# A position-bias table made in five steps instead of two, its rows repeated from DRAM instead of from SBUF

## The chip, the cores and the metric

The kernel runs on one core of a Trainium2 chip. The metric is the device time of one execution in microseconds (us); less is better. A measurement is the median of several executions, and beside it one execution was recorded by the hardware profiler. Engines are named as in the profile: PE (matrix products), PEld (its weight loads), DVE (vector), ACT (scalar), POOL (GpSimd), SP (the queue from which every transfer of this kernel is issued).

## The reference

Two layers on one sequence of 256 positions with 2048 features, all in float32. Layer 0 mixes the positions with an RWKV-7 recurrence, layer 1 with a causal differential attention of 8 heads; behind each mixer stands a gated MLP of width 5504 with a short convolution on its gate. After every part the input is scaled, added and normalised. The attention adds to its scores a bias that depends only on the distance of query and key:

```python
dist = (start + jnp.arange(Q_BLOCK))[:, None] - k_pos[None, :]
bias = jnp.transpose(rel_bias[rel_bucket(dist)], (2, 0, 1))
s = s + bias[None, :, None].astype(jnp.float32)
s = jnp.where(dist >= 0, s, -1e30)
```

`rel_bias` has 32 rows (buckets of distance) and 8 columns (heads).

```python
def conv_glu(x, w_up, conv_w, conv_b, w_down):
    u, g = jnp.split(x @ w_up, 2, axis=-1)
    ...
    return (u * jax.nn.gelu(gc)) @ w_down
```

## The kernel before

Activations stand transposed: a feature block of 128 lies on the partitions, the 256 positions along them, so `X` is 16 blocks of 128x256 (`KT` = 16). The order of the parts is fixed: RWKV, first MLP (`glu(0)`), attention, second MLP. Weights are read from DRAM once, in blocks made on the host so that one output block's weights are contiguous.

**A product.** `dense` makes one output block. Its weights come in transfers of four 128x128 tiles, `raw` (L204, 128 rows of 2 KB). ACT rounds two tiles at a time to a short format (`hi`, L210), DVE takes the rest (`lo`, L213), and PE multiplies each tile twice (L225 with `hi`, 512 columns; L226 with `lo`, 256 columns). In the MLP there are two pools in turn, each with 3 buffers for `raw`, 4 for `hi` and 4 for `lo`: that is how far the loads can run ahead of PE. SP issues a `raw` when the buffer that it goes into has been read by ACT and DVE.

**The MLP.** The first product (`ff_up`) makes the 43 blocks of `hs`. The second (`ff_down`) is the loop at L553: for j = 0 to 15 one output block of 43 tiles, taken in by `ln_add`, which adds it to `X` and starts the normalisation. After the first two blocks a mean is taken on PE (L394).

**The bias table.** `bias_table` is a generator that the loop advances by one step before block 1 and before block 4. It loads constants (`ext`, L173, and `rel`, L583). One small product on PE (L585) makes `tab`, 8 rows (one a head) of 384 values, one for each distance; DVE copies it from PSUM (L587). Then every row is written 128 times into the DRAM tile `dtab` (L590), and the table `B` is read back with a step of 383 between partitions (L593), which turns each repeated row into a matrix that is skewed by one position from partition to partition. The first step ends here. The second makes the small factors `nlam` and `sub` (a product at L599, an exponential at L601). The attention reads `B` at L653.

**What sets the order.** The kernel is written with a framework that places tiles, makes every semaphore and orders the instructions of each engine: program order is the priority, but an instruction whose inputs and buffers are ready can be put ahead of one that is not. On SP all instructions are carried out in the order so found, and one that waits holds up those behind it.

Of the kernel before, what the change touches and what calls it, by code (L numbers as in the profile page):

```python
# [8 lines left out]
F32 = mybir.dt.float32  # L9
# [5 lines left out]
P = 128  # L15
# [5 lines left out]
NH = 8  # L21
# [104 lines left out]
class Trunk:  # L126
# [374 lines left out]
    def glu(self, i, lead, ahead=None, out=None):  # L501
        nc, tc = self.nc, self.tc
        with ExitStack() as ctx:
            self.weight_pools(ctx, f"g{i}")
            self.psum_pool(ctx, f"g{i}", 5)
            hp = ctx.enter_context(tc.tile_pool(name=f"glu_h{i}", bufs=1))
            gp_ = ctx.enter_context(tc.tile_pool(name=f"glu_t{i}", bufs=2))
            hs = hp.tile([P, FT, 2 * T], F32R, name="hs")
            gps = [hp.tile([P, T + 2], F32, name=f"gp{k}") for k in range(2)]
            for g in gps:  # L510
                nc.gpsimd.memset(g[:, 0:2], 0.0)
            cpar = hp.tile([P, 4 * FT], F32, name="cpar")
            nc.sync.dma_start(out=cpar, in_=self.a["par"][:, PCOL[f"cw{i}0"]:PCOL[f"cw{i}0"] + 4 * FT])
            cw = lambda k, j: cpar[:, k * FT + j:k * FT + j + 1]
            state = {}

            def evac(idx, ps):
                j = idx // 2
                if idx % 2 == 0:
                    g = gps[j % 2]  # L520
                    self.total(ps, g[:, 2:])
                    gc = gp_.tile([P, T], F32, name="gc")
                    nc.vector.tensor_scalar(out=gc, in0=g[:, 0:T], scalar1=cw(0, j),
                                            scalar2=cw(3, j), op0=ALU.mult, op1=ALU.add)
                    for k in (1, 2):
                        nc.vector.scalar_tensor_tensor(out=gc, in0=g[:, k:k + T], scalar=cw(k, j),
                                                       in1=gc, op0=ALU.mult, op1=ALU.add)
                    nc.scalar.activation(out=gc, in_=gc, func=AF.Gelu_apprx_tanh)
                    state[j] = gc
                else:  # L530
                    u = gp_.tile([P, T], F32, name="u")
                    self.total(ps, u)
                    nc.vector.tensor_tensor(out=u, in0=u, in1=state.pop(j), op=ALU.mult)
                    self.split(u, hs[:, j, :])

            blocks = self.up_blocks(i)
            n = 0
            if lead:
                n = len(lead.src)
                rest = lead.run(evac, [self.psum() for _ in lead.src])  # L540
                next(rest)
                if LEAD["e"] == 0:
                    _all(rest)
            for j, w in enumerate(blocks[n:]):
                def ev(_, ps, j=j):
                    if lead:
                        for _ in range(LEAD["e"]):
                            next(rest, None)
                    evac(j + n, ps)
                self.dense([w], KT, self.S0, ev)  # L550
            todo = self.bias_table() if i == 0 else iter(())
            self.ln_begin(ahead)
            for j in range(KT):  # L553
                if j in (1, 4):
                    next(todo, None)
                last = j == KT - 1
                self.dense([self.a["ff_down"][i][j]], FT, hs, lambda _, ps: self.ln_add(j, ps, narrow=last, last=last),
                           narrow=last)
            if out is not None:
                self.ln_stats()  # L560
                self.ln_finish(i, 1, out)
            elif not ahead:
                self.ln_plain(i, 1)
# [12 lines left out]
    def bias_table(self):  # L576

        nc, tc = self.nc, self.tc
        with tc.tile_pool(name="bt", bufs=1) as bp, tc.tile_pool(name="bd", bufs=1, space=bass.MemoryType.DRAM) as dp:
            self.extra(bp, CRW, NCONST)  # L580
            rel = bp.tile([NB + 1, NH], F32, name="rel")
            nc.gpsimd.memset(rel[NB:NB + 1, :], -1e30)
            nc.sync.dma_start(out=rel[:NB, :], in_=self.a["rel_bias"])  # L583
            ps = self.psum()
            nc.tensor.matmul(ps[:NH, :384], lhsT=rel, rhs=self.x("onehot", 384, NB + 1), start=True, stop=True)  # L585
            tab = bp.tile([NH, 384], F32, name="tab")
            nc.vector.tensor_copy(out=tab, in_=ps[:NH, :384])  # L587

            dt = dp.tile([NH, P, 384], F32, name="dtab")
            nc.sync.dma_start(out=dt, in_=tab.unsqueeze(1).broadcast_to([NH, P, 384]))  # L590
            src = dt[:, :, :]
            skew = bass.AP(src.tensor, src.offset + P - 1, [[383, P], [P * 384, NH], [1, T]])
            nc.sync.dma_start(out=self.B, in_=skew)  # L593
            yield
            lp = bp.tile([P, 2], F32, name="lp")
            lam = self.p("lam", 0, 4).rearrange("p (a b) -> p a b", b=2)
            nc.vector.tensor_tensor(out=lp, in0=lam[:, :, 0], in1=lam[:, :, 1], op=ALU.mult)
            ps = self.psum()
            nc.tensor.matmul(ps[:, :2], lhsT=self.x("ones"), rhs=lp, start=True, stop=True)  # L599
            le = bp.tile([P, 2], F32, name="le")  # L600
            nc.scalar.activation(out=le, in_=ps[:, :2], func=AF.Exp)  # L601
            nc.vector.tensor_tensor(out=self.nlam, in0=le[:, 1:2], in1=le[:, 0:1], op=ALU.subtract)
            nc.vector.tensor_scalar(out=self.nlam, in0=self.nlam, scalar1=LAMBDA_INIT, scalar2=None,
                                    op0=ALU.subtract)
            nc.vector.tensor_scalar(out=self.sub, in0=self.p("subln", 0, 2), scalar1=1.0 - LAMBDA_INIT,
                                    scalar2=None, op0=ALU.mult)
# [317 lines left out]
def _all(steps):  # L924
    for _ in steps:
        pass
# [531 lines left out]
```

## Time and profile before

| | |
|---|---|
| median of 3 executions | 2594.23 us (2592.02 to 2599.16) |
| profiled execution, its own time | 2589.51 us |
| its span in the profile | 2587.7 us |
| PE busy / DVE / ACT / POOL | 95% / 79% / 64% / 15% of the span |
| DMA, mean over the span | 166 GB/s |

The span runs from the first to the last recorded instruction; the execution's own time has 1.8 us more around it. Start times in the rows are microseconds from the start of the span.

### The profile page before, as it was taken

The numbers are of one execution on the slowest core, as the hardware profiler recorded it, in microseconds if no ns is written. First come the engines' busy times: TensorE is split into PE (matmuls) and PEld (weight loads), VectorE is DVE, ScalarE is ACT, GpSimd is POOL, SyncE is SP. The second block draws the span as 40 slices with busy tenths as digits, with TensorE's granted clock in tenths as the row PEclk, the third lists the DMA queues.
The fourth block names the chain that finished last, engine by engine and source line by source line (L and its number), as shares of the span: only waits on it lengthen the run. The fifth ranks groups of instructions, "written<-read, shape, count | busy, mean of one in ns | idle before, by whom it ended". The sixth has DMA issues, their size and how long they took to land.

```text
span 2587.7 us, 54801 instructions
## 1 busy us (share of the span) xinstructions
PE 2469.0 (95%) x17598; PEld 2173.1 (84%) x17598; DVE 2056.9 (79%) x5100; ACT 1643.8 (64%) x4319; POOL 391.0 (15%) x456
## 2 busy tenths in 40 slices
PE   7998899999899999996999999999999999999996
PEld 6887788777788888885888999998888888888886
DVE  8988978887997777774777877779997777777776
ACT  5766556645676666663666666666676666666664
POOL 4343334332300000000111200002300000000111
PEclk9999989899999999998999999999999999999998
DMA  5544334344365555556666455556465555566664
GB/s 189 175 131 124 104 95 116 85 134 126 119 205 190 189 190 189 190 189 137 199 189 187 149 177 171 168 167 197 146 194 187 188 188 188 188 188 186 190 189 127
DMA packets 285161, 429.61 MB, mean 166 GB/s; under 512 B 69064, under 2 KB 91592, under 8 KB 284872
## 3 DMA queue, kind: packets, MB, share of 16 engines
q1 hardware_dynamic: 284872, 426.12, 54.8%
q8 instruction: 137, 2.24, 0.3%
q14 instruction: 152, 1.25, 0.2%
HBM read 419.45 MB, written 6.56 MB: 165 GB/s over the span
## 4 chain that ended last, share of the span: by engine, by line
PE 79%; DVE 5%; DMA 2%; issue 1%; ACT 1%; POOL 0%; DVEq 0%; ACTq 0%; SPq 0%; POOLq 0%
PE psd L225 41%; PE psd L226 21%; PE psd L221 2%; PE psd L223 2%; PE psd L222 2%; DMA dtab<-tab 1%; PE psd L293 1%; PE psd L291 1%; PE psd L292 1%; DVE lo L213 1%; PE psd L891 1%; PE psd L890 1%; PE psd L892 1%; PE lnst L345 1%; PE pss L1136 0%
## 5 line engine op out<-in xcount | busy, mean ns | idle before, releaser
L210 ACT CAST hi<-raw 128x256 fp32r<-128x256 f32 (+1 forms) x3128 | 1228.8, 404 | 698.2 <-PE psd L225 475.1
L213 DVE TENSOR_TENSOR lo<-raw,hi 128x256 fp32r<-128x256 f32 (+1 forms) x2984 | 1291.3, 442 | 418.4 <-ACT hi L210 383.4
L225 PE MATMUL psd<-S,hi 128*128 128x512 f32 x3004 | 1058.8, 396 | 0.1
L226 PE MATMUL psd<-S,lo 128*128 128x256 f32 x3004 | 843.2, 281 | 3.4 <-DVE lo L213 3.2
L225 PEld LDWEIGHTS psd<-S,hi 128*128 128x128 f32 x3004 | 567.1, 189 | 132.6 <-ACT hi L210 1.1
L226 PEld LDWEIGHTS psd<-S,lo 128*128 128x128 f32 x3004 | 566.7, 189 | 5.4 <-DVE lo L213 4.1
L225 PE MATMUL psd<-hs,hi 128*128 128x512 f32 x1290 | 452.4, 394 | 22.7 <-ACT hi L210 22.7
L226 PE MATMUL psd<-hs,lo 128*128 128x256 f32 x1290 | 362.3, 281 | 0.8 <-DVE lo L213 0.8
L225 PEld LDWEIGHTS psd<-hs,hi 128*128 128x128 f32 x1290 | 242.5, 188 | 79.0 <-ACT hi L210 23.5
L226 PEld LDWEIGHTS psd<-hs,lo 128*128 128x128 f32 x1290 | 243.8, 189 | 1.7 <-DVE lo L213 1.6
L363 POOL COPY ln_acc<-X 128x256 f32<-128x256 f32 x4 | 2.1, 527 | 1258.2 <-DVE X L397 1258.2
L213 POOL TENSOR_TENSOR lo<-raw,hi 128x256 fp32r<-128x256 f32 x144 | 132.9, 929 | 297.3 <-ACT hi L210 226.7
L223 PE MATMUL psd<-S,lo 128*128 128x256 f32 x480 | 140.2, 292 | 14.3 <-DVE lo L213 8.9
L222 PE MATMUL psd<-S,hi 128*128 128x256 f32 x480 | 142.0, 296 | 0.0
L221 PE MATMUL psd<-S,hi 128*128 128x256 f32 x480 | 140.8, 293 | 0.5 <-ACT hi L210 0.5
L223 PEld LDWEIGHTS psd<-S,lo 128*128 128x128 f32 x480 | 92.5, 193 | 23.3 <-DVE lo L213 13.4
L225 PE MATMUL psd<-S1r,hi 128*128 128x512 f32 x276 | 109.0, 424 | 1.6 <-ACT o_rs L1043 0.7
L370 POOL TENSOR_TENSOR ln_acc<-ln_acc,X 128x256 f32<-128x256 f32 x49 | 40.1, 818 | 402.5 <-DVE X L409 402.2
L221 PEld LDWEIGHTS psd<-S,hi 128*128 128x128 f32 x480 | 92.1, 192 | 4.4 <-ACT hi L210 0.8
L222 PEld LDWEIGHTS psd<-S,hi 128*128 128x128 f32 x480 | 92.5, 193 | 3.6 <-issue 3.4
L221 PE MATMUL psd<-S1r,hi 128*128 128x256 f32 x284 | 86.7, 305 | 0.9 <-ACT S1r L191 0.9
L891 PE MATMUL psd<-S,lo 128*128 128x258 f32 x256 | 76.7, 299 | 9.8 <-DVE lo L213 9.8
(298 smaller groups left out, 3818.5 us busy)
## 6 DMA issues: line engine op xcount, KB each, us to landing
raw<-in_ff_up SPq DMA_DIRECT2D x676, 256.0 KB, 3.4
raw<-in_ff_down SPq DMA_DIRECT2D x320, 256.0 KB, 3.0
raw<-in_rkv SPq DMA_DIRECT2D x192, 256.0 KB, 3.5
raw<-in_da_qk SPq DMA_DIRECT2D x122, 256.0 KB, 3.4
raw<-in_da_v SPq DMA_DIRECT2D x64, 256.0 KB, 3.0
raw<-in_da_o SPq DMA_DIRECT2D x64, 256.0 KB, 3.5
raw<-in_rw_o SPq DMA_DIRECT2D x50, 256.0 KB, 3.5
raw<-in_ff_down SPq DMA_DIRECT2D x32, 192.0 KB, 2.5
```

The source lines that it names most:

```text
L210: nc.scalar.copy(out=hi[:, :s * P], in_=r)
L213: eng.tensor_tensor(out=lo[:, :s * P], in0=r, in1=hi[:, :s * P].bitcast(F32), op=ALU.subtract)
L221: nc.tensor.matmul(ps[:, :T], lhsT=hi, rhs=xs[:, :T], start=first, stop=False)
L222: nc.tensor.matmul(ps[:, :T], lhsT=hi, rhs=xs[:, T:], start=False, stop=False)
L223: nc.tensor.matmul(ps[:, :T], lhsT=lo, rhs=xs[:, :T], start=False, stop=last)
L225: nc.tensor.matmul(ps, lhsT=hi, rhs=xs, start=first, stop=False)
L226: nc.tensor.matmul(ps[:, T:], lhsT=lo, rhs=xs[:, :T], start=False, stop=last)
L291: nc.tensor.matmul(o, lhsT=xh, rhs=hi, start=k == 0 and b == 0, stop=False)
L292: nc.tensor.matmul(o, lhsT=xh, rhs=lo, start=False, stop=False)
L293: nc.tensor.matmul(o, lhsT=xl, rhs=hi, start=False, stop=k == KT - 1 and b == T // P - 1)
L370: nc.gpsimd.tensor_tensor(out=self.ln_acc[:, hs], in0=self.ln_acc[:, hs], in1=t, op=ALU.add)
L891: nc.tensor.matmul(ps[:, 2:4 + T], lhsT=lo[:, w], rhs=x[:, 2:4 + T], start=False, stop=False)
```

## The change

The generator is advanced before blocks 1, 3, 5, 7 and 9 and has five steps: the loads of the constants; the product, the copy and a write of the 8 rows of `tab`, once, into a new DRAM tile `drow`; the repetition, now from `drow` in DRAM into `dtab` in DRAM, with the 128 copies as the outermost dimension of the transfer on both sides; the skewed read of `B`; and the factors `nlam` and `sub`.

```diff
-                if j in (1, 4):
+                if j in (1, 3, 5, 7, 9):
                     next(todo, None)
...
             nc.sync.dma_start(out=rel[:NB, :], in_=self.a["rel_bias"])
+            yield
             ps = self.psum()
...
             nc.vector.tensor_copy(out=tab, in_=ps[:NH, :384])
+            d0 = dp.tile([NH, 384], F32, name="drow")
+            nc.sync.dma_start(out=d0, in_=tab)
+            yield
 
             dt = dp.tile([NH, P, 384], F32, name="dtab")
-            nc.sync.dma_start(out=dt, in_=tab.unsqueeze(1).broadcast_to([NH, P, 384]))
+            nc.sync.dma_start(out=dt.rearrange("h p m -> p h m"),
+                              in_=d0.unsqueeze(1).broadcast_to([NH, P, 384]).rearrange("h p m -> p h m"))
+            yield
             src = dt[:, :, :]
             skew = bass.AP(src.tensor, src.offset + P - 1, [[383, P], [P * 384, NH], [1, T]])
             nc.sync.dma_start(out=self.B, in_=skew)
```

## Rows read from the trace of the kernel before

**Rows 1.** The page: span, PE's busy time, and the ending chain by line.

```profile
span 2587.7 us, 54801 instructions
PE 2469.0 (95%) x17598; PEld 2173.1 (84%) x17598; DVE 2056.9 (79%) x5100; ACT 1643.8 (64%) x4319; POOL 391.0 (15%) x456
...
PE psd L225 41%; PE psd L226 21%; PE psd L221 2%; PE psd L223 2%; PE psd L222 2%; DMA dtab<-tab 1%; PE psd L293 1%; PE psd L291 1%; PE psd L292 1%; DVE lo L213 1%; PE psd L891 1%; PE psd L890 1%; PE psd L892 1%; PE lnst L345 1%; PE pss L1136 0%
```

**Rows 2.** Chain that ended last, 1178 to 1235: start, us, what.

```profile
1181.90 34.27 DMA dtab<-tab
...
1216.67 5.73 DMA raw<-in_ff_down
```

**Rows 3.** PE's waits, 1175 to 1230: total, times, longest.

```profile
PE psd L225 <- ACT hi L210: 22.7, 1, 22.7
PE psd L226 <- DVE lo L213: 0.8, 2, 0.6
```

**Rows 4.** Timeline of PE: start, us, instruction, [idle before it <- releaser].

```profile
1191.13 0.40 PE L225 MATMUL psd<-hs,hi 128*128 128x512 f32 x1
...
1191.48 0.39 PE L225 MATMUL psd<-hs,hi 128*128 128x512 f32 x1
...
1193.93 0.59 PE L394 MATMUL psd<-X,cst 128*128 128x256 f32 x2
1194.36 0.28 PE L599 MATMUL psd<-lp,ext 128*128 128x2 f32 x2
1217.37 0.79 PE L225 MATMUL psd<-hs,hi 128*128 128x512 f32 x1 [22.73 <-ACT hi L210]
...
1220.77 0.41 PE L225 MATMUL psd<-hs,hi 128*128 128x512 f32 x1
```

**Rows 5.** Timeline of DVE: the sums that take in blocks 0, 2 and 3.

```profile
1180.90 0.41 DVE L387 SCALAR_TENSOR_TENSOR X<-X,psd 128x256 f32<-128x256 f32 x1
...
1238.76 0.41 DVE L406 TENSOR_TENSOR t<-t,psd 128x256 f32<-128x256 f32 x1
...
1253.81 0.41 DVE L406 TENSOR_TENSOR t<-t,psd 128x256 f32<-128x256 f32 x1
```

**Rows 6.** Busy by stretch; the last three columns are PE's clock, DMA share, GB/s.

```profile
1160.00:1180.00 20.00, 20.00 (x116) 17.49 (x115) 13.96 (x37) 12.75 (x33) 0.00 (x0) 1.00 0.66 186
1184.00:1186.00 2.00, 2.00 (x13) 1.76 (x12) 1.22 (x3) 1.20 (x3) 0.00 (x0) 1.00 0.46 49
1198.00:1200.00 2.00, 0.00 (x0) 0.00 (x0) 0.00 (x0) 0.00 (x0) 0.00 (x0) 0.50 0.60 98
1218.00:1226.00 8.00, 8.00 (x40) 7.01 (x39) 5.25 (x14) 4.30 (x14) 1.49 (x3) 0.83 1.02 352
2580.00:2582.00 2.00, 0.00 (x0) 0.00 (x0) 2.00 (x6) 2.00 (x6) 0.00 (x0) 0.50 0.92 338
```

**Rows 7.** Timeline of SP, 1181 to 1217.

```profile
1182.83 18.83 SPq L204 DMA_DIRECT2D raw<-in_ff_down  x3
1216.19 0.38 SPq L593 DMA_DIRECT2D B<-dtab  x1
```

**Rows 8.** What SP waited for, 1232 to 1440: total, times, longest.

```profile
SPq L204 <- DVE lo L213: 129.2, 130, 2.4
```

**Rows 9.** DMA issues: count, KB each, us from issue to landing.

```profile
out_y<-X SPq DMA_DIRECT2D x8, 256.0 KB, 2.1
...
d<-Tl SPq DMA_DIRECT2D x16, 32.0 KB, 3.2
```

**Rows 10.** By tile, `rel` and `B`: ns min/median/max, first and last start.

```profile
L585 PE MATMUL psd<-ext,rel x2: 482/484/486, 1180.5 to 1180.8; 33*8 33x384 f32 x2
L583 SPq DMA_DIRECT2D rel<-in_rel_bias x1: 423/423/423, 632.9 to 632.9; - x1
...
L653 DVE SCALAR_TENSOR_TENSOR s<-pss,B x16: 417/551/692, 1483.9 to 1732.3; 128x256 f32<-128x256 f32 x8, 128x512 f32<-128x512 f32 x8
```

**Rows 11.** Timeline of ACT: the table load ahead of L601.

```profile
1188.84 1.28 ACT L601 ACT_TABLE_LOAD   x1
```

## The prediction

> **What bounds the kernel now.** I read the page first: PE is busy for 95% of the span and the ending chain is nearly all its products, so only what makes PE idle or slow is worth time; one entry there is a transfer, `dtab<-tab`, with 1% [rows 1]. The chain around it shows where that entry comes from: 34.27 us from the issue at L590 to its end, and then 5.73 us of a weight load that had to follow [rows 2]. The waits of PE tell what it costs there: one wait of 22.7 us on a weight tile, and two short ones on `lo` [rows 3]. The timeline of PE gives the place: after L599 at 1194.36 the next product starts at 1217.37 [rows 4].
>
> The stretches tell why weights were missing. Before the table the loads take 0.66 of the 16 DMA engines and 186 GB/s; after L590 the engines are still 0.46 busy but move 49 GB/s [rows 6]. The transfer is 8 x 128 x 384 x 4 = 1.57 MB, so in 34.27 us it moves 46 GB/s: nearly half of the engines are held by one slow transfer, and each `raw` behind it is spread over all of them. SP issued three more `raw` (the issues alone took 18.83 us) and then stood at L593 until 1216.19 [rows 7]. So weights that PE needed waited behind the table.
>
> **What the stall costs.** Three terms. (1) PE's idle time, 22.73 us [rows 4]. [...] Five tiles take 1220.77 - 1217.37 = 3.40 us; at the pitch of 0.35 us between two L225 at 1191 they would take 1.75 [rows 4]: 1.65 us. (3) The two waits on `lo`, 0.8 us by the waits [rows 3]. Together 25.2 us. As a check: from the sum after block 0 to that after block 2 are 1238.76 - 1180.90 = 57.9 us, and one block is 1253.81 - 1238.76 = 15.05 [rows 5]; the excess over two blocks is 27.8. In it lie L585 with two passes of 0.48, L394 twice with 0.59 and L599 with 0.28 [rows 4, 10], 2.4 us of work that stays: 25.4 us remain. Both ways agree.
>
> **The change part by part.**
>
> The cover. L590 was issued at 1181.90 and PE had weights until L394 at 1193.93 [rows 4]: 12.0 us. Nothing that SP or the DMA engines are held up by for less than that reaches PE. In the steady loop SP waits for `lo` to free a buffer, in 130 waits over 208 us [rows 8], so the buffers are full when a table transfer comes; I take 12.0 us for each.
>
> Loads of `ext` and `rel`: they stay in the first step. L583 ran at 632.9, long before block 1 [rows 10], so instructions move ahead of their place when their inputs are ready. Cost nothing, as now.
>
> L585 and the copy move from block 1 to block 3 at the same price. The new write of `drow` is 12 KB in 8 rows. The nearest row, 32 KB to DRAM, lands in 3.2 us [rows 9]; its bounds are 0 and those 3.2. I take 3.2, under the cover of 12.0: nothing. If the next transfer is put in the queue too early, SP stands for no more than that, with the raws behind it, under the same cover.
>
> The repetition is the disputed part, and no transfer from DRAM to DRAM stands in the trace. From below: the best stretch, loads and the read of `B`, moved 352 GB/s at a share of 1.02 [rows 6], so 1.57 MB take 4.5 us. A store to DRAM at 0.92 moved 338 GB/s [rows 6], 4.7 us, so DRAM as a destination isn't slow. From above: the transfer of now, 34.3 us [rows 2]. I take load plus store, as if they did not overlap: 9.2 us. It is nearest to the store, which also uses rows of 1 to 2 KB and all engines, since the 128 copies are now the outermost dimension. 9.2 is under 12.0: nothing on PE, and 25.2 us of gain.
>
> Why the transfer of now is slow isn't seen in the rows: it could be its source of 8 partitions, its outermost dimension of 8, or its rows of 1.5 KB. [...]
>
> The read of `B` moves behind the repetition as now. Its 128 x 8 x 256 x 4 = 1.05 MB at 352 GB/s are 3.0 us. Between the two, SP and the engines serve raws at a share of 0.66 [rows 6], so the lateness shrinks by a third of the time. At worst the read comes at once: 9.2 + 3.0 = 12.2 us, and 2.1 us of landing [rows 9] for which SP stands at L593, 14.3 against 12.0. So PE may idle 0 to 2.3 us; I take 0. `B` is first read at 1483.9 [rows 10]; block 9 starts some 120 us after block 1, by 1320, so even without moving ahead it is ready in time.
>
> The factors. L599 runs in the loop either way. L601's table load takes ACT 1.28 us [rows 11]; at block 9 it may fall away or stay, hidden by 16 ready `hi` tiles of 0.35 us. 0 to 1.3 us; I take 0. POOL is touched by nothing here.
>
> **The sum.** Removed 25.2 us, added nothing that PE sees. On the profiled execution's own time 2589.5 - 25.2 = 2564.3 us. The median shown is 4.7 us above that execution, so on the median 2594.2 - 25.2 = 2569 us.
>
> **Rivals.**
>
> (a) The stall goes, as above: 2569, 2562 to 2576 with the 0 to 3.6 us above, a reordered loop, and the spread of the runs shown (7 us). Chance 0.70. For it: the cover, and stores that reach 338 GB/s. Against it: no row of this kind of copy.
>
> (b) A row of 1.5 KB costs an engine what it does now. Eight engines write 128 rows each, 34.27 / 128 = 0.268 us a row. On 16 engines 64 rows are 17.1 us. PE idles 17.1 - 12.0 = 5.1 us, then 3.0 for `B` without cover, then 1.65 of slow clock: 9.8 lost, 15.4 gained, 2579 us. For it: the transfer of now has the same rows. Against: `raw` and the store have rows of 2 KB and run seven times as fast. Chance 0.14.
>
> (c) The rate stays at 46 GB/s, because many copies of a small source are what is slow, and the change doesn't do what it says. 34.3 - 12.0 + 3.0 + 1.65 = 27.0 us lost against 25.2: 2596, within the bound. Chance 0.07.
>
> (d) The other side. All 16 engines now read the same 12 KB of DRAM, in the same order, and if that place delivers no more than one engine's part of the best stretch, 352 / 16 = 22 GB/s, the repetition takes 71.5 us. 71.5 - 12.0 + 3.0 + 1.65 = 64.2 lost against 25.2: 39 us slower, 2633. It decides from a repetition of 33 us on. For it: no load of the trace takes one place again and again. Against: 12 KB are 8 rows, which the engines may reach at different moments. Chance 0.06. [...]
>
> (e) 0.03 for a loop whose new order costs 5 us or more elsewhere, between (a) and no change.
>
> **Range and chances.** 0.3% (7.8 us) is about what a measurement of this kernel can tell from no change: faster is below 2586.4. (a), (b) and most of (e) are faster, 0.86; (c) and part of (e) the same, 0.08; (d) slower, 0.06. The range takes (a) and (b) with a few us around (b): 2562 to 2583, and leaves out some 0.16 of the upper cases and little below.
>
> **What would show it.** Right: no wait of PE over 3 us in the second product of the first MLP, a granted clock of 1.00 through it, blocks of 15.05 us throughout but for L585 and L394, no transfer of the table in the ending chain, and a stretch of a few us near block 3 in which DMA is full and moves over 300 GB/s, reads and writes counted once. The three transfers stand in SP's queue with raws between, even if all come within block 3 or 4. Wrong: a stretch of low GB/s and half-busy engines longer than 12 us behind the repetition ((b) to (d), told apart by its length of 17, 34 or 70 us), or SP standing at L593 with PE out of weights, or a new wait in another stage.

## The result, and the profile after

The changed kernel takes 2569.11 us (median of 4 executions, 2567.62 to 2570.56), the kernel before 2594.02 (also of 4, 2592.02 to 2599.16). The ratio is 0.9891, with a 95% interval of 0.9876 to 0.9905: faster, by 24.9 us between the medians, where 25.2 were forecast (2569 us).

The page of the changed kernel answers to [rows 1]: the span is 21.2 us shorter, PE's busy time is the same, and the transfer of the table is no longer in the ending chain.

```profile
span 2566.5 us, 54810 instructions
PE 2468.5 (96%) x17598; PEld 2171.5 (85%) x17598; DVE 2053.8 (80%) x5100; ACT 1645.2 (64%) x4318; POOL 390.7 (15%) x456
...
PE psd L225 42%; PE psd L226 21%; PE psd L293 1%; PE psd L291 1%; PE psd L292 1%; DVE lo L213 1%; PE psd L897 1%; PE psd L896 1%; PE psd L898 1%; PE lnst L345 1%; PE psd L221 1%; PE psd L223 1%; PE psd L222 1%; DMA raw<-in_rw_o 0%; PE pss L656 0%
```

The spans differ by less than the medians because the two recorded executions differ ahead of the change. The sum after block 0 (L387 in the timeline of DVE) starts at 1185.64 in the changed kernel and at 1180.90 in the one before [rows 5], 4.7 us later, although up to block 1 every engine has the same instructions in the same order in both. So the stage itself is compared, from that sum to the first instruction of POOL behind the second product (L435). After, in the timelines of DVE and POOL:

```profile
1185.64 0.41 DVE L387 SCALAR_TENSOR_TENSOR X<-X,psd 128x256 f32<-128x256 f32 x1
...
1423.16 13.73 POOL L435 TENSOR_TENSOR X<-X,ln_dm 128x256 f32<-128x256 f32 x16 [21.67 <-ACT ln_dm L420]
```

And its end in the timeline of POOL of the kernel before:

```profile
1443.53 13.74 POOL L435 TENSOR_TENSOR X<-X,ln_dm 128x256 f32<-128x256 f32 x16 [21.67 <-ACT ln_dm L420]
```

The stage took 1443.53 - 1180.90 = 262.63 us and takes 1423.16 - 1185.64 = 237.52: 25.1 us less.

The timeline of SP shows the new transfers. L594 and L599 are issued at 1221.05 and 1234.05, so they moved ahead of blocks 5 and 7: at that time PE is at blocks 3 and 4.

```profile
1217.51 0.34 SPq L590 DMA_DIRECT2D drow<-tab  x1
1218.18 2.82 SPq L204 DMA_DIRECT2D raw<-in_ff_down  x2
1221.05 0.61 SPq L594 DMA_DIRECT2D dtab<-drow  x1
1221.75 12.25 SPq L204 DMA_DIRECT2D raw<-in_ff_down  x8
1234.05 0.43 SPq L599 DMA_DIRECT2D B<-dtab  x1
```

The part of the page on DMA issues has their time to landing in its last column:

```profile
dtab<-drow SPq DMA_DIRECT2D x1, 1536.0 KB, 9.2
...
B<-dtab SPq DMA_DIRECT2D x1, 1024.0 KB, 7.3
```

The stretches (columns as in [rows 6]) answer to the stalled ones there. All 16 engines work at 320 GB/s where 8 worked at 49, and the granted clock stays at 1.00:

```profile
1221.00:1224.00 3.00, 3.00 (x19) 2.62 (x18) 2.16 (x6) 1.64 (x4) 0.00 (x0) 1.00 0.56 162
1224.00:1232.00 8.00, 8.00 (x47) 6.87 (x46) 2.19 (x6) 2.16 (x6) 0.00 (x0) 1.00 0.99 320
1232.00:1234.00 2.00, 1.93 (x11) 1.37 (x10) 1.79 (x6) 2.00 (x8) 0.00 (x0) 1.00 0.46 157
1234.00:1262.00 28.00, 28.00 (x163) 24.55 (x162) 20.95 (x52) 17.19 (x48) 4.13 (x4) 1.00 0.78 249
```

The timeline of PE in the third stretch shows how close it was. At 1232.23 a product starts 0.58 us after the one before it, and the next 0.69 after that, where 0.35 is the pitch: 0.57 us lost in all.

```profile
1231.65 0.40 PE L225 MATMUL psd<-hs,hi 128*128 128x512 f32 x1
1231.88 0.28 PE L226 MATMUL psd<-hs,lo 128*128 128x256 f32 x1
1232.23 0.50 PE L225 MATMUL psd<-hs,hi 128*128 128x512 f32 x1
1232.69 0.39 PE L226 MATMUL psd<-hs,lo 128*128 128x256 f32 x1
1232.92 0.39 PE L225 MATMUL psd<-hs,hi 128*128 128x512 f32 x1
```

ACT had stood idle for 4.65 us. Its row names PE as the releaser, but what came late were the weights: the nine `raw` of four tiles issued from 1221 to 1235 took 7.5 us to land in the median, where those of the whole execution took 3.0. The rows of ACT and of the DMA issues:

```profile
1231.78 3.17 ACT L210 CAST hi<-raw 128x256 fp32r<-128x256 f32 x10 [4.65 <-PE psd L225]
...
raw<-in_ff_down SPq DMA_DIRECT2D x9, 256.0 KB, 7.5
```

### The profile page after: what moved, and what is told of

Same layout as the page of the kernel before. It is cut to its first block, busy times and chain, and to the rows that moved or that the text cites. A ratio compares the mean times of both kernels' runs of the same rounds, so it can differ in the third digit from the quotient of the medians.

```text
span 2566.5 us, 54810 instructions
## 1 busy us (share of the span) xinstructions
PE 2468.5 (96%) x17598; PEld 2171.5 (85%) x17598; DVE 2053.8 (80%) x5100; ACT 1645.2 (64%) x4318; POOL 390.7 (15%) x456
## 4 chain that ended last, share of the span: by engine, by line
PE 74%; DVE 4%; ACT 1%; issue 1%; DMA 1%; POOL 0%; ACTq 0%; DVEq 0%; SPq 0%; POOLq 0%
PE psd L225 42%; PE psd L226 21%; PE psd L293 1%; PE psd L291 1%; PE psd L292 1%; DVE lo L213 1%; PE psd L897 1%; PE psd L896 1%; PE psd L898 1%; PE lnst L345 1%; PE psd L221 1%; PE psd L223 1%; PE psd L222 1%; DMA raw<-in_rw_o 0%; PE pss L656 0%
```

## The experiments

The change does three things at once: it spreads the steps, it takes the rows from DRAM, and it puts the copies outermost. The first two kernels part the spreading from the transfers.

**Steps only.** The five steps, with the old transfer (edit of the changed kernel, one line cut short):

```diff
-            d0 = dp.tile([NH, 384], F32, name="drow")
-            nc.sync.dma_start(out=d0, in_=tab)
             yield
             dt = dp.tile([NH, P, 384], F32, name="dtab")
-            nc.sync.dma_start(out=dt.rearrange("h p m -> p h m"), ...)
+            nc.sync.dma_start(out=dt, in_=tab.unsqueeze(1).broadcast_to([NH, P, 384]))
```

> The five steps of the change, with the repetition of the kernel before: from the 8 rows in SBUF, heads outermost, no row table in DRAM. My theory (the stall goes because the transfer got shorter than the cover of the weight buffers; where the steps stand does not matter): the repetition still takes about 34 us, PE idles 20 to 25 us in block 3 instead of block 1, and the ratio to the kernel before is 0.998 to 1.002. Rival (the spreading over five steps took the wait out of SP's queue): PE idles less than 5 us, ratio 0.989 to 0.992.

The ratio is 0.9994 (0.9981 to 1.0008). The stall has moved from block 1 to block 3 and is as long as it was; the waits of PE from 1215 to 1280:

```profile
PE psd L225 <- ACT hi L210: 23.2, 1, 23.2
```

Here the read of `B` was issued at 1263.1, long after the repetition had ended, so SP didn't stand at it. PE idled all the same: the weight load that SP issued right behind the repetition took 34.03 us to land (the chain from 1215 to 1275). So it was late in the DMA engines, not behind a waiting instruction. My theory holds, the rival falls.

```profile
1220.95 34.03 DMA raw<-in_ff_down
```

**Transfers only.** The two steps of before, with the transfers of the change in the first (edit of the kernel before):

```diff
+            d0 = dp.tile([NH, 384], F32, name="drow")
+            nc.sync.dma_start(out=d0, in_=tab)
             dt = dp.tile([NH, P, 384], F32, name="dtab")
-            nc.sync.dma_start(out=dt, in_=tab.unsqueeze(1).broadcast_to([NH, P, 384]))
+            nc.sync.dma_start(out=dt.rearrange("h p m -> p h m"),
+                              in_=d0.unsqueeze(1).broadcast_to([NH, P, 384]).rearrange("h p m -> p h m"))
```

> The two steps of the kernel before, with the transfers of the change: row table to DRAM, repetition from DRAM with the copies outermost, read of B, all in the step ahead of block 1. My theory: the repetition lands in 9 to 11 us, PE idles 0 to 3 us although the read of B stands only a few weight loads behind the repetition, ratio 0.988 to 0.991. Rival (the five steps matter): SP stands at the read of B and PE runs dry for 8 us or more, ratio 0.994 to 1.000.

The ratio is 0.9900 (0.9867 to 0.9934), and the stage takes 236.96 us, no longer than in the changed kernel. The repetition landed after 8.7 us, a little sooner than expected. SP did stand at the read of `B`, three weight loads behind the repetition; what SP waited for, 1187 to 1252:

```profile
SPq L204 <- DVE lo L213: 35.7, 39, 3.2
SPq L596 <- DMA dtab<-drow: 4.5, 1, 4.5
```

PE had no wait in that window. Together the two kernels show that the five steps bring nothing that these measurements can tell; the transfers bring it all.

**Heads outer.** The changed kernel, but the repetition runs over the heads first, as before:

```diff
-            nc.sync.dma_start(out=dt.rearrange("h p m -> p h m"),
-                              in_=d0.unsqueeze(1).broadcast_to([NH, P, 384]).rearrange("h p m -> p h m"))
+            nc.sync.dma_start(out=dt, in_=d0.unsqueeze(1).broadcast_to([NH, P, 384]))
```

> The changed kernel, but the repetition has the 8 heads outermost again, as in the kernel before; its source stays in DRAM. If the source in SBUF was what made it slow: 8 engines at the price of a row in the changed kernel, some 7 us for 64 rows, so 128 rows in 14 us and 2 us of landing: 16 us, half of the engines busy, PE idles 4 to 8 us, ratio 0.991 to 0.994. If the outermost dimension of 8 with the price of a row as before (0.268 us) was it: 34 us, PE idles 20 us or more, ratio 0.998 to 1.002.

The ratio is 0.9926 (0.9906 to 0.9946). A stretch in which the engines moved almost only the repetition, by microsecond:

```profile
1233.00:1234.00 1.00, 1.00 (x8) 0.88 (x7) 0.68 (x2) 0.42 (x3) 0.00 (x0) 1.00 0.53 194
1234.00:1235.00 1.00, 1.00 (x8) 0.86 (x7) 0.59 (x2) 0.70 (x2) 0.00 (x0) 1.00 0.56 206
```

Half of the engines are busy, as in the stalled stretch of before [rows 6], but they move some 200 GB/s and not 49. The last rows of the table are written by 1241, some 11 us after the issue at 1229.7, where 16 were expected. From 1241 to 1244 half of the engines are still as busy (shares of 0.47 to 0.55), but with weights: in the DMA view of these 3 us no packet has the table's 1.5 KB. The 38 under 2 KB are all under 512 B, and the others are rows of 2 KB:

```profile
DMA packets 326, 0.59 MB, mean 197 GB/s; under 512 B 38, under 2 KB 38, under 8 KB 326
```

So a part of the weight loads came last, I take it the part that lay behind the table on the same engines (the view names no engine), and PE waited:

```profile
PE psd L225 <- ACT hi L210: 2.0, 1, 2.0
PE psd L226 <- DVE lo L213: 0.7, 1, 0.7
```

That is less than the 4 us expected, but the stage is 241.55 us, 4.0 more than in the changed kernel, since the granted clock fell to 0.50 after the idle time (it was 0.65 as the mean of 1245 to 1249):

```profile
1245.00:1246.00 1.00, 1.00 (x5) 0.81 (x4) 1.00 (x5) 0.25 (x1) 0.00 (x0) 0.50 0.48 82
```

So in this place 8 engines instead of 16 cost 4 us, and the 8 rows in SBUF as the source the other 21; what it was about that source that made the transfer slow, the next kernel tries.

**Spread rows.** The kernel before, with the 8 rows of `tab` on partitions 0, 4, 8 to 28:

```diff
-            nc.tensor.matmul(ps[:NH, :384], lhsT=rel, ...)
-            tab = bp.tile([NH, 384], F32, name="tab")
+            wide = bp.tile([NB + 1, 4 * NH], F32, name="wide")
+            nc.gpsimd.memset(wide, 0.0)
+            nc.gpsimd.tensor_copy(out=wide[:, 0:4 * NH:4], in_=rel)
+            nc.tensor.matmul(ps[:4 * NH, :384], lhsT=wide, ...)
+            tab = bp.tile([4 * NH, 384], F32, name="tab")
...
-            nc.sync.dma_start(out=dt, in_=tab.unsqueeze(1).broadcast_to([NH, P, 384]))
+            nc.sync.dma_start(out=dt, in_=tab[0:4 * NH:4].unsqueeze(1).broadcast_to([NH, P, 384]))
```

> The kernel before, with one thing different: the 8 rows lie on partitions 0, 4, 8 to 28 instead of 0 to 7 (a zero-filled factor of 32 columns in the small product, and a copy on POOL). Heads outermost, two steps, source in SBUF, rows of 1,536 bytes as before. [...] If the rows' length, the 8 engines or SBUF as such were it: 34 us as before, ratio 0.998 to 1.002.

The ratio is 0.9918 (0.9895 to 0.9940). The chain from 1182 to 1215 answers to [rows 2]: 11.43 us where 34.27 stood.

```profile
1184.90 11.43 DMA dtab<-tab
...
1196.82 5.68 DMA raw<-in_ff_down
```

The stretches by microsecond show half of the engines busy, as before, at four times the rate (in these 2 us they move rows of the table alone):

```profile
1187.00:1188.00 1.00, 1.00 (x7) 0.90 (x6) 0.73 (x2) 0.50 (x2) 0.00 (x0) 1.00 0.54 203
1188.00:1189.00 1.00, 1.00 (x7) 0.88 (x7) 0.50 (x2) 0.72 (x2) 0.00 (x0) 1.00 0.54 203
```

The repetition's 11.43 us are far from the 34 of before, and fewer even than the 14 to 18 that I had estimated for 8 engines at about the price of a row in the changed kernel; PE waited 1.4 us in all, not the 4 to 9 that went with them. Nothing is different here but the partitions of the source (and a wider small product with its copy on POOL): not the number of engines, not the rows' length, not the memory. The slow thing before was that eight engines read eight neighbouring partitions. The packets in the traces say the same row by row: a row of the table takes 228 ns before, with never more than eight under way while the table alone is moved, and 65 ns in the changed kernel. The stretches shown give 65 ns for spread rows (1.5 KB at 203 GB/s on 0.54 of 16 engines) and 67 for heads outer (at 194 to 206 GB/s on 0.53 to 0.56).

**Twice.** The changed kernel with 256 copies of each row in the one transfer; the second half is never read.

```diff
-            dt = dp.tile([NH, P, 384], F32, name="dtab")
+            dt = dp.tile([NH, 2 * P, 384], F32, name="dtab")
...
-                              in_=d0.unsqueeze(1).broadcast_to([NH, P, 384]).rearrange("h p m -> p h m"))
+                              in_=d0.unsqueeze(1).broadcast_to([NH, 2 * P, 384]).rearrange("h p m -> p h m"))
...
-            skew = bass.AP(src.tensor, src.offset + P - 1, [[383, P], [P * 384, NH], [1, T]])
+            skew = bass.AP(src.tensor, src.offset + P - 1, [[383, P], [2 * P * 384, NH], [1, T]])
```

> The changed kernel with 256 copies of each row instead of 128 in the one repetition (3.15 MB; the second half is never read). My theory: the cover is some 11 to 12 us and all of it is used by the changed kernel, so the added 1.57 MB at the rate measured for it (7 us) come out as PE's idle time nearly whole: the repetition lands in 16 to 17 us, PE idles 5 to 9 us with the slow restart, ratio to the kernel before 0.991 to 0.994, that is 5 to 11 us over the changed kernel. Rival (weight loads and the repetition share the engines, so a longer one only thins the loads out): PE idles less than 2 us, ratio 0.988 to 0.9905.

The ratio is 0.9948 (0.9929 to 0.9967), a little above the range expected, whose upper end lies inside the interval; the repetition lands in 15.0 us, sooner than the 16 to 17 expected. The timeline of PE:

```profile
1239.15 0.28 PE L226 MATMUL psd<-hs,lo 128*128 128x256 f32 x1
1245.29 0.79 PE L225 MATMUL psd<-hs,hi 128*128 128x512 f32 x1 [5.87 <-ACT hi L210]
```

Landing grew by 5.8 us, PE idles 5.87, and the stage takes 245.26 us, 7.7 more than in the changed kernel: the idle time and the slow restart. Issued at 1228.3, out of weights at 1239.4: the cover was 11.1 us. What is added beyond the changed kernel's 9.2 us reaches PE whole, so that kernel uses up the cover, although 9.2 is less than 11.1: from the landing, at 1243.4, to the first product, at 1245.29, pass another 1.9 us, in which the last of the weights land and are rounded.

**All partitions.** Two steps, no row table in DRAM. The small product gives each head's row on 16 partitions, and each of the 128 partitions is written 8 times.

```diff
+            wide = bp.tile([NB + 1, NH, 16], F32, name="wide")
+            nc.gpsimd.tensor_copy(out=wide, in_=rel.unsqueeze(2).broadcast_to([NB + 1, NH, 16]))
...
-            nc.sync.dma_start(out=dt, in_=tab.unsqueeze(1).broadcast_to([NH, P, 384]))
+            nc.sync.dma_start(out=dt.rearrange("h (r i) m -> (h r) i m", i=8),
+                              in_=tab.unsqueeze(1).broadcast_to([P, 8, 384]))
```

> Two steps as in the kernel before and no row table in DRAM: the small product gives each head's row on 16 partitions (a factor of 128 columns, spread by a copy on POOL), and the repetition goes from all 128 partitions of SBUF, 8 copies from each. If source partitions and engines were the whole cause, SBUF as a source is as good as DRAM: the repetition lands in 6 to 10 us, PE idles less than 1.5 us, ratio 0.987 to 0.991, no different from the changed kernel. If a source in SBUF is slow as such for repeated rows: 17 us or more, PE idles over 4 us, ratio 0.992 or more.

The ratio is 0.9902 (0.9869 to 0.9934). The issues from 1190 to 1210:

```profile
dtab<-tab SPq DMA_DIRECT2D x1, 1536.0 KB, 6.9
```

SBUF is no slower a source than DRAM when all partitions give: 6.9 us against 8.7 to 9.2, with one transfer less. The stage, 237.46 us, is no shorter, since nothing was left to gain on PE.

**The changed kernel again**, beside the last two:

> The changed kernel once more, beside the two others on the same chip: ratio 0.988 to 0.991, the repetition landing in 9 us, PE idle for less than 1 us in block 3.

The ratio is 0.9912 (0.9882 to 0.9942), the repetition landed in 8.7 us, and PE had no wait around it.

The kernels by stage (L387 to L435, from one profile each) and by time:

| | stage, us | repetition, us | ratio to before |
|---|---|---|---|
| before | 262.63 | 34.3 | 1 |
| steps only | 261.95 | some 34 | 0.9994 |
| twice | 245.26 | 15.0 | 0.9948 |
| heads outer | 241.55 | some 11 | 0.9926 |
| spread rows | 239.78 | 11.4 | 0.9918 |
| all partitions | 237.46 | 6.9 | 0.9902 |
| transfers only | 236.96 | 8.7 | 0.9900 |
| changed, first and again | 237.52, 236.93 | 9.2, 8.7 | 0.9891, 0.9912 |

The last three rows can't be told apart by time. Heads outer and spread rows are told from them by their stages alone, each from one profile (the changed kernel's own two differ by 0.6 us); the intervals of the ratios overlap. No version beat the changed kernel.

## Why the prediction was right, point by point

**What the stall costs** (25.2 us): the stage got 25.1 us shorter. Of the three terms, the idle time of 22.73 us is gone; the slow restart of 1.65 is gone, since the clock stays at 1.00 through the stage, where before it was 0.50 in the idle time and 0.83 as the mean of 1218 to 1226 [rows 6]; and PE has no wait on `lo` in it. The check beside the sum agrees less closely than it says: the row of L394, 0.59 us, is that of both its products (x2), so 1.8 us of work stay and not 2.4, and 26.0 us remain against 25.2.

**The cover** (12.0 us) was right as a mechanism, with steps only and twice as its two sides, and 0.9 us too long: 11.1 us in twice. It took the buffers to be full at every issue. By the loads that SP had issued and the tiles that PE had multiplied, 35 tiles of 0.35 us were ahead of PE at the issue in the kernel before and 31 in twice and in the changed kernel, one `raw` less. Block 3 as such isn't the reason: in steps only, issued there too, 35 were ahead, and PE had weights from 1220.0 to 1232.3. Nor is the write of `drow` by itself: in transfers only, with that write in block 1, 35 were ahead as well. In the changed kernel SP issued only two `raw` from 1217.5 to 1221 and had waits for the sums of block 2 on DVE; that these cost the one `raw` was not tried.

**The comparison of landing and cover** left a term out. The prediction saw 12.0 - 9.2 = 2.8 us to spare. There was nothing to spare: of the 11.1 us, 9.2 went to the landing and, as twice shows, 1.9 to what has to follow it before PE can go on, and PE did lose 0.57 us. That it lost no more is luck too.

**The repetition** was taken at 9.2 us and landed after 9.2, but that the two agree is luck. I had added load and store as if they did not overlap. In fact the engines moved 320 GB/s, raws and repetition together, at a share of 0.99, close to the best rate of before (352 at 1.02), and in heads outer the repetition almost by itself moved 194 to 206 GB/s at 0.53 to 0.56: load and store overlap, and the rest of the 9.2 us is raws on the same engines and the landing. Twice the size took 5.8 us more, which is 271 GB/s for the added 1.57 MB with raws beside it.

**The read of `B`** (0 to 2.3 us on PE, 0 taken): it cost PE nothing to be seen, even in transfers only, where SP stood 4.5 us at it. The 0.57 us that PE lost in the changed kernel came before the read was issued.

**The factors** cost nothing: L601's exponential runs as L607 at 1308.1, at the end of block 8, and its table load is gone from ACT's list.

**The rivals.** (b), a price that goes with rows of 1.5 KB, falls with spread rows: the same rows from SBUF, on the same number of engines, in a third of the time. What the prediction held against it was weaker than it reads: the loads ran seven times as fast on twice the engines, so by the engine 352 / 16 = 22 GB/s against 49 / 8 = 6.1, under four times. (c) and (d), a small source that is slow to read many times, fall with the changed kernel itself: 1.57 MB in 9.2 us are 171 GB/s, the waiting and the raws on the same engines included.

These 171 GB/s are over seven times the 22 that (d) took for the one place; how the 12 KB lie in DRAM no run shows.

For the old source, the experiment that changes only the partitions measured 49 GB/s from partitions 0 to 7 and 203 from partitions 0, 4, 8 to 28. So the limit went with the neighbouring partitions. What it is in them no run shows, nor how much the spread ones could give: eight engines moved as much from DRAM in heads outer (194 to 206), so they may be the limit themselves.

What the prediction left open, whether source, outermost dimension or rows made the transfer slow, is now shared out: source partitions some 21 to 23 us of the stage, 8 engines in place of 16 the other 2 to 4 (2 in block 1, with 35 tiles ahead, 4 in block 3 with 31). The rows of 1.5 KB were the same in every kernel, and slow only from the 8 neighbouring partitions, so the slowness wasn't theirs.

## What to carry to other kernels

A transfer of the side work needn't be waited for by anyone to stall a kernel: here it was enough that it held 8 of the 16 DMA engines for some 34 us, longer than the 12.0 to 12.3 us that the weights in the buffers of the main loop lasted. Read that cover off the trace (from the issue of the long transfer to the last product with weights), compare it with the landing time and with what follows the landing before the next product (1.9 us here), and shorten the transfer before moving it: moving it only moved the stall here (23.2 us in block 3 in place of 22.7 in block 1). A table that is made on a few partitions is worth spreading over more before it is copied out repeatedly: here 8 neighbouring partitions took 34.3 us, 8 that lie 4 apart 11.4, and all 128 took 6.9, for one wider small product and a copy on POOL.

## What the runs showed of the hardware that was not expected

- Eight engines, busy for much the same share (0.45 to 0.56), moved 49 GB/s from 8 neighbouring partitions (228 ns a row of 1.5 KB) and some 200 GB/s from 8 partitions that lie 4 apart (65 ns), and as much from DRAM (67 ns in heads outer). So the busy share of the engines alone doesn't show that a transfer is held up at its source; share and GB/s have to be read together.
- Twelve KB of DRAM read 128 times by 16 engines gave no sign of a crowded place: at least 171 GB/s for this transfer alone, 320 with the raws beside it.
- The transfer that kept half of the engines in heads outer made the loads late in part only: its rows were written by 1241, and for another 3 us half of the engines, still at some 200 GB/s, moved weights.
